# Activations computed in their result tiles, forget gates started five steps later, projection banks six and mixed banks two

## The chip, the cores and the metric

The kernel runs on one core of one Trainium2 chip. The metric is the device time of one execution in microseconds (us): the median of several executions, here 3062.44 us over three (3062.06 to 3065.12). A profiled execution is a run of its own and has its own time.

## What is computed

Two layers of a hybrid model on one sequence of 1024 tokens of width 2048, all in fp32. One layer, cut to what matters:

```python
mod = silu(c) @ w_mod + b_mod                      # shift, scale, gate
h = rms_norm(x, g_pre) * (1 + scale) + shift
proj = h @ w_in                                    # a_q a_k a_v | s_u s_v | c_q c_k c_v c_g | z
y_a = sliding_window_attention(rope(a_q), rope(a_k), a_v, sinks)    # 16 heads of 64, 4 of keys
y_b = chunked_spatial_gating(gelu(s_u), gelu(s_v), ...)             # 8 groups, chunks of 128
log_alpha = log_sigmoid(c_g @ gla_w_gate_up + gla_b_gate) / 16      # the forget gates
y_c = rms_norm(gated_linear_attention(c_q, c_k, c_v, log_alpha))    # 4 heads
y = concat(y_a, y_b, y_c) * silu(z)
x = x + gate * rms_norm(y @ w_out, g_post)
```

`gelu` is the tanh form; `silu(z)` is computed as z (1 + tanh(z/2)) / 2, with the factor of a half put elsewhere.

## The kernel before

**Phases.** There are four phases, one for each of the two layers and the two halves of the sequence (512 tokens): `in_phase` computes the projections and all mixers of a half, `out_phase` the output projection. The time is set by TensorE (PE), which runs the projections as three matmuls for one product: weights and activations are each split into a rounded high part and the rest, and high by high, high by rest and rest by high are summed in one PSUM bank (`mm_f`, L378, with the features on the partitions; `mm_t`, L386, with the tokens). Each group of projections (`group`, L394) has four result tiles of 128 x 512, each with a PSUM bank of its own from the pool `pj`, and runs over the 16 blocks of the inner dimension: for each block, one step of three matmuls into each of the four tiles. A group has 64 such steps. The order of the groups in a phase is `kcq`, `ck`, `vcg`, `q0`, `cv`, `q1`, `zc`, `sv`, `su`, `zb`, `za0`, `za1` and then four of the output; the first phase computes `kcq` and `ck` in a stage of its own at the start, together with the modulation vector.

**Weights.** Each weight block is loaded by a DMA of the SP queue, cast to its high part on ScalarE (ACT, L368), and the rest is taken on VectorE (DVE, L369); `w_take` keeps some blocks ready ahead.

**Lanes.** All else is written as generators that stand in lanes named `mod`, `att`, `gla`, `sg` and `fin`. After each projection step `tick` (L82) is called, and each lane whose time has come goes on to its next `yield`; the number it yields says after how many ticks it is called again. So a lane's matmuls are laid between those of the projections:
- `gla` first takes the forget gates (`gates`, L566): four transposes of the `c_g` columns of the value tiles (L569), a copy (L571), two matmuls (L576) and the elementwise work; then `gla_scores` (L593), twice, with small matmuls that fill two mixed banks at once (`far` at L649 with L655, `near` at L633) and are read by predicated copies (L620); then `gla_blocks` (L697: L712 and L715 into one bank, L722 into another); then the output transposes (L559).
- `att` takes four pairs of heads twice in a phase (`attention`, L473): two score tiles at once (L490), read by a ScalarE copy (L499, or L497 at the start of the sequence) and a predicated VectorE copy (L500), then softmax (L505 to L519), transposes (L532), and the product with the values (L546).
- `sg` mixes the gated part (L892); `mod` computes the modulation of what is to come during the first two phases.

All these matmuls write banks of the pool `mx`. PSUM has eight banks in this kernel, five for `pj` and three for `mx`.

**Order.** The order of instructions on each engine is not that of the source. A planner at compile time simulates the engines, and at each moment gives an engine the earliest instruction in the source whose inputs and tile it believes ready; `urgent` and `high_priority` move instructions ahead in this. A pool with n buffers gives out n tiles; the next one waits until one is released by its last reader. On the chip each engine then takes its own instructions strictly in the planned order, and waits where the planner was too hopeful.

**Activations.** After a group the results leave PSUM by `evac` (L761, copies on ScalarE, L767), `silu2` (L425) or `gelu2` (L431). The last two compute with scratch tiles of the pool `t2`, which has four buffers and serves many others as well (the rotary tables, gates, residual rows). Results go into tiles of the pool `hold`, which has 16 buffers, or, for `zb`, into a `t2` tile.

Of the kernel before, what the change touches and what calls it, by code (L numbers as in the profile page):

```python
# [15 lines left out]
AF = mybir.ActivationFunctionType  # L16
ALU = mybir.AluOpType
AX = mybir.AxisListType
PSUM = bass.MemoryType.PSUM
# [20 lines left out]
def hybrid_kernel(ctx: ExitStack, tc: tile.TileContext, a, y_out):  # L40
# [6 lines left out]
    whl_p = ctx.enter_context(tc.tile_pool(name="whl", bufs=4))  # L47
    t2_p = ctx.enter_context(tc.tile_pool(name="t2", bufs=4))
    sm = ctx.enter_context(tc.tile_pool(name="sm", bufs=2))
    pj = ctx.enter_context(tc.tile_pool(name="pj", bufs=5, space=PSUM))  # L50
    mx = ctx.enter_context(tc.tile_pool(name="mx", bufs=3, space=PSUM))
    pools = {}

    V, S, G, PE = nc.vector, nc.scalar, nc.gpsimd, nc.tensor

    def load(out, in_):
        nc.sync.dma_start(out=out, in_=in_)

    def urgent():
        return tc.high_priority(offset=PRIO)  # L60
# [32 lines left out]
    def hold(shape=(P, 512), dt=F32):  # L93
        return pools["hold"].tile(list(shape), dt, tag="hold", name="hold")

    def t2(shape=(P, 512), dt=F32):
        return t2_p.tile(list(shape), dt, tag="t2", name="t2")
# [7 lines left out]
    def mxt():  # L105
        return mx.tile([P, 512], F32, tag="mx", name="mx")

    def pjt():
        return pj.tile([P, 512], F32, tag="pj", name="pj")
# [13 lines left out]
    def rsqrt(out, src, n, pool=sm):  # L123

        i = pool.tile([P, n], I32, tag="rq_i", name="rq_i")
        V.tensor_scalar(i, src.bitcast(I32), 1, None, ALU.logical_shift_right)
        V.tensor_scalar(i, i, -1.0, 1597463007.0, ALU.mult, ALU.add)
        yv = i.bitcast(F32)
        for it in range(3):
            w = pool.tile([P, n], F32, tag="rq_w", name="rq_w")  # L130
            V.tensor_tensor(w, yv, yv, ALU.mult)
            V.scalar_tensor_tensor(w, w, -0.5, src, ALU.mult, ALU.mult)
            dst = out if it == 2 else yv
            V.scalar_tensor_tensor(dst, w, 1.5, yv, ALU.add, ALU.mult)
            yv = dst
# [288 lines left out]

    def silu2(dst, ps):  # L425

        t = t2()
        S.activation(t, ps, AF.Tanh, scale=0.5)
        V.scalar_tensor_tensor(dst, t, 1.0, ps, ALU.add, ALU.mult)

    def gelu2(dst, ps):  # L431

        x = t2()
        u = t2()
        with urgent():
            S.copy(x, ps)  # L436
        S.activation(u, x, AF.Square)
        V.tensor_scalar(u, u, 0.044715, 1.0, ALU.mult, ALU.add)
        V.tensor_tensor(u, u, x, ALU.mult)
        S.activation(u, u, AF.Tanh, scale=GELU_C)  # L440
        V.scalar_tensor_tensor(dst, u, 1.0, x, ALU.add, ALU.mult)

    y_d = [[dram.tile([P, 512], F32, name=f"y{h}_{j}") for j in range(NK)] for h in range(NH)]
    state = {}
# [119 lines left out]
            yield 3  # L564

    def gates(l, cg):  # L566
        tp = mxt()
        for n in range(NT):
            PE.transpose(tp[0:16, n * P:(n + 1) * P], cg[n], ident)  # L569
        cgT = t2()[32 * l:32 * l + 16, :]  # L570
        S.copy(cgT, tp[0:16, :])  # L571
        yield 9
        bs = []
        for i in range(2):
            ps = mxt()
            PE.matmul(ps, lhsT=wup[l][:, i * P:(i + 1) * P], rhs=cgT, start=True, stop=True)  # L576
            mn = t2()
            V.tensor_scalar(mn, ps, bgate[l][:, i:i + 1], 0.0, ALU.add, ALU.min)
            ab = t2()
            S.activation(ab, ps, AF.Abs, bias=bgate[l][:, i:i + 1])  # L580
            S.activation(ab, ab, AF.Exp, scale=-1.0)
            S.activation(ab, ab, AF.Ln, bias=1.0)
            V.scalar_tensor_tensor(mn, mn, CAP, ab, ALU.max, ALU.subtract)
            b = hold()
            for n in range(NT):
                c = slice(n * P, (n + 1) * P)
                V.tensor_tensor_scan(b[:, c], ones, mn[:, c], 0.0, ALU.mult, ALU.add)
            bs.append(b)
            yield 4
        yield 8  # L590
        return bs
# [162 lines left out]
    def in_phase(l, h, slots, pre=None):  # L754
# [61 lines left out]
        for n in range(NT):  # L816
            t = hold()
            with urgent():
                silu2(t, ps[n])
            zt.append(t)  # L820
# [14 lines left out]
        for n in range(NT):  # L835
            vn.append(hold())
            gelu2(vn[n], ps[n])
# [176 lines left out]
    with tc.tile_pool(name="start", bufs=1) as st:  # L1014

        load(mb[0], a["b_mod_col"][0])
        load(gpc[0], a["g_pre"][0])
        xq = [act_p.tile([P, 2, H], F32, tag="act", name="xq") for _ in range(8)]
        for c in range(8):
            load(xq[c], a["x_f"][0, 2 * c:2 * c + 2].rearrange("j p t -> p j t"))  # L1020
        scb = st.tile([P, NK, 32], F32, name="scb")
        V.tensor_copy(scb, sc.unsqueeze(2).broadcast_to([P, NK, 32]))
        ws, raw_q, hl_q = deque(), deque(), deque()

        def first_load(k):
            if k < NK:
                r = wraw_p.tile([P, 1, 768], F32, tag="wraw", name="wraw")
                load(r[:, 0, 0:512], a["w_in"][0, 0, :, k])
                load(r[:, 0, 512:], a["w_ck"][0, :, k])
                raw_q.append(r)  # L1030

        def first_split():
            r = raw_q.popleft()
            hl = whl_p.tile([P, 2, 1, 768], F32R, tag="whl", name="whl")
            S.copy(hl[:, 0], r)
            V.tensor_tensor(hl[:, 1], r, hl[:, 0].bitcast(F32), ALU.subtract)
            hl_q.append(hl)

        def mod_load(c, part):
            if c < 8:  # L1040
                w = st.tile([P, 8, 512], F32, name="wm0", bufs=3)
                load(w, a["w_mod"][0, c, :, 8 * part:8 * part + 8])
                ws.append(w)
        mod_load(0, 0)
        mod_load(0, 1)
        mod_load(1, 0)
        first_load(0)


        sums = mxt()  # L1050
        for c in range(8):
            sq = st.tile([P, 2, H], F32, name="sq", bufs=2)
            S.activation(sq, xq[c], AF.Square)
            s2 = st.tile([P, H], F32, name="s2", bufs=2)
            V.tensor_tensor(s2, sq[:, 0], sq[:, 1], ALU.add)
            PE.matmul(sums, lhsT=ones, rhs=s2, start=(c == 0), stop=(c == 7))
        r0 = st.tile([P, H], F32, name="r0")
        V.tensor_scalar(r0, sums, 1.0 / D, EPS, ALU.mult, ALU.add)
        rsqrt(r0, r0, H, st)
        psk = [mxt()] + [pjt() for _ in range(5)]  # L1060

        def project(k):
            first_split()
            if k >= NK - 2:
                w_load()
            hl = hl_q.popleft()
            for m in range(6):
                mm_f(psk[m], hl, 0, m, slots[k], k)

        def mod_products(mps, part):  # L1070

            w = ws.popleft()
            for kk in range(8):
                k = 8 * part + kk
                r = 32 * (k % 4)
                PE.matmul(mps[r:r + 32, :], lhsT=scb[:, k], rhs=w[:, kk], start=(k < 4), stop=(k >= 12))  # L1076

        def fill(c, mps):
            acc = st.tile([P, 512], F32, name="mod_acc", bufs=2)
            S.copy(acc, mps)  # L1080
            mod_columns(0, c, acc, 4)
            for j in range(2):
                k = 2 * c + j
                xt, b = t2(), bcol[0][:, k:k + 1]
                V.scalar_tensor_tensor(xt, xq[c][:, j], acol[0][:, k:k + 1], r0, ALU.mult, ALU.mult)
                s = act_p.tile([P, 2, 512], F32R, tag="act", name="act")
                S.activation(s[:, 0], xt, AF.Identity, bias=b)
                V.scalar_tensor_tensor(s[:, 1], xt, b, s[:, 0].bitcast(F32), ALU.add, ALU.subtract)
                slots.append(s)

        for c in range(8):
            if c:
                mod_load(c, 1)
                first_load(2 * c - 1)
            mps = mxt()
            mod_products(mps, 0)
            if c:
                project(2 * c - 2)  # L1100
                mod_load(c + 1, 0)
                first_load(2 * c)
            mod_products(mps, 1)
            with urgent():
                fill(c, mps)
            if c:
                project(2 * c - 1)
            if c == 5:
                for _ in rope_tables(0):
                    pass  # L1110
        first_load(NK - 1)
        project(NK - 2)
        project(NK - 1)
        w_split()
        w_split()
# [147 lines left out]
```

## Time and profile before

| | |
|---|---|
| time, median of 3 | 3062.44 us (3062.06 to 3065.12) |
| the profiled execution's own time | 3067.03 us |
| its span, first to last instruction | 3065.3 us |
| mean granted clock of TensorE | 0.993 |
| TensorE busy | 3000.0 us (98%), 17298 matmuls |
| VectorE busy | 1840.3 us (60%) |
| ScalarE busy | 1229.8 us (40%) |

In the profile PE is TensorE's matmuls and PEld its weight loads, DVE is VectorE, ACT is ScalarE, POOL is GpSimd and SP issues the DMAs. L382 is line 382 of the kernel before. A row of the waits names the instruction that waited, what it waited for, and the total, the number and the longest of these waits. A row of the timeline has the start, the duration, the engine and its instruction, `out<-in` by tile pool, and in brackets the idle time of the engine just before and what ended it. A row of one line's instructions has their shortest, median and longest duration in ns. A matmul's record lasts longer than the time to the next one, since matmuls overlap.

### The profile page before, as it was taken

The numbers are of one execution on the slowest core, as the hardware profiler recorded it, in microseconds if no ns is written. First come the engines' busy times: TensorE is split into PE (matmuls) and PEld (weight loads), VectorE is DVE, ScalarE is ACT, GpSimd is POOL, SyncE is SP. The second block draws the span as 40 slices with busy tenths as digits, with TensorE's granted clock in tenths as the row PEclk, the third lists the DMA queues.
The fourth block names the chain that finished last, engine by engine and source line by source line (L and its number), as shares of the span: only waits on it lengthen the run. The fifth ranks groups of instructions, "written<-read, shape, count | busy, mean of one in ns | idle before, by whom it ended". The sixth has DMA issues, their size and how long they took to land.

```text
span 3065.3 us, 44211 instructions
## 1 busy us (share of the span) xinstructions
PE 3000.0 (98%) x17298; PEld 2440.8 (80%) x17298; DVE 1840.3 (60%) x2948; ACT 1229.8 (40%) x2415; POOL 24.5 (1%) x66
## 2 busy tenths in 40 slices
PE   8999999999998999999999999999999999999998
PEld 4678777888886888788888788888888888888886
DVE  4668778464767877644364766644346476663425
ACT  3355455232434544323243554423223455442322
POOL 0000000000000000000000000000000000000000
PEclk9999999999999999999999999999999999999999
DMA  9744457475784445544455223334446322343535
GB/s 394 276 138 152 141 179 224 131 243 158 223 255 154 129 138 184 164 126 141 123 159 163 83 73 100 121 114 144 120 124 192 106 83 83 114 133 105 165 103 162
DMA packets 214914, 468.98 MB, mean 153 GB/s; under 512 B 21008, under 2 KB 72624, under 8 KB 212656
## 3 DMA queue, kind: packets, MB, share of 16 engines
q1 hardware_dynamic: 214704, 466.15, 48.6%
q8 instruction: 136, 2.23, 0.3%
q14 instruction: 74, 0.61, 0.1%
HBM read 429.37 MB, written 36.70 MB: 152 GB/s over the span
## 4 chain that ended last, share of the span: by engine, by line
PE 81%; DVE 8%; DMA 6%; ACT 3%; issue 2%; SPq 0%; DVEq 0%; ACTq 0%
PE pj L382 12%; PE pj L390 12%; PE pj L392 12%; PE pj L383 12%; PE pj L384 12%; PE pj L391 12%; DMA wm<-in_w_mod_dram 3%; PE mx L490 2%; PE mx L546 2%; DVE whl L369 2%; DVE ma L225 1%; PE mx L532 1%; ACT whl L368 1%; PE mx L1076 1%; DMA t<-in_x_dram 1%
## 5 line engine op out<-in xcount | busy, mean ns | idle before, releaser
L369 DVE TENSOR_TENSOR whl<-wraw,whl 128x1024 fp32r<-128x1024 f32 (+2 forms) x504 | 587.3, 1166 | 720.9 <-ACT whl L368 719.9
L368 ACT CAST whl<-wraw 128x1024 fp32r<-128x1024 f32 (+2 forms) x504 | 505.0, 1002 | 1048.3 <-PE pj L392 494.6
L390 PE MATMUL pj<-whl,act 128*128 128x512 f32 (+1 forms) x2048 | 785.0, 383 | 0.5 <-ACT hold L767 0.5
L392 PE MATMUL pj<-whl,act 128*128 128x512 f32 (+1 forms) x2048 | 778.5, 380 | 0.0
L391 PE MATMUL pj<-whl,act 128*128 128x512 f32 (+1 forms) x2048 | 775.9, 379 | 0.0
L382 PE MATMUL pj<-act,whl 128*128 128x512 f32 x1904 | 756.4, 397 | 9.1 <-ACT t L436 8.2
L383 PE MATMUL pj<-act,whl 128*128 128x512 f32 x1904 | 744.2, 391 | 0.0
L384 PE MATMUL pj<-act,whl 128*128 128x512 f32 x1904 | 742.6, 390 | 0.0
L392 PEld LDWEIGHTS pj<-whl,act 128*128 128x128 f32 x2048 | 385.6, 188 | 72.2 <-issue 0.3
L390 PEld LDWEIGHTS pj<-whl,act 128*128 128x128 f32 x2048 | 386.3, 189 | 70.8 <-issue 2.5
L391 PEld LDWEIGHTS pj<-whl,act 128*128 128x128 f32 x2048 | 386.0, 188 | 67.0 <-issue 0.8
L382 PEld LDWEIGHTS pj<-act,whl 128*128 128x128 f32 x1904 | 358.5, 188 | 100.4 <-issue 14.3
L384 PEld LDWEIGHTS pj<-act,whl 128*128 128x128 f32 x1904 | 358.6, 188 | 76.5
L383 PEld LDWEIGHTS pj<-act,whl 128*128 128x128 f32 x1904 | 358.9, 188 | 70.7 <-issue 0.7
L225 DVE SCALAR_TENSOR_TENSOR ma<-wm,sc,ma 128x512 f32<-128x512 f32 x240 | 179.9, 750 | 61.6 <-DMA wm<-in_w_mod_dram 58.7
L516 ACT ACTIVATE M<-M,at_nm 128x128 f32<-128x128 f32 x256 | 99.6, 390 | 19.4 <-DVE at_nm L508 19.4
L535 DVE TENSOR_TENSOR PT<-mx,amask 128x1024 f32<-128x1024 f32 x64 | 77.8, 1221 | 17.1 <-PE mx L532 17.0
L500 DVE COPY_PREDICATED M<-pmask,mx 128x256 f32<-128x256 uint8 x128 | 51.2, 442 | 53.5 <-ACT M L499 41.5
L490 PE MATMUL mx<-kc,qs 128*128 128x256 f32 (+1 forms) x256 | 66.2, 288 | 10.5 <-DVE hold L620 5.9
L490 PE MATMUL mx<-kc,qlo 128*128 128x256 f32 (+1 forms) x256 | 65.8, 285 | 0.0
L499 ACT COPY M<-mx 128x256 f32<-128x256 f32 x96 | 31.7, 375 | 80.7 <-PE mx L490 80.7
L490 PEld LDWEIGHTS mx<-kc,qs 128*128 128x128 f32 x256 | 49.3, 193 | 17.7 <-issue 7.1
(230 smaller groups left out, 2390.1 us busy)
## 6 DMA issues: line engine op xcount, KB each, us to landing
wraw<-in_w_in_dram SPq DMA_DIRECT2D x312, 512.0 KB, 3.6
wraw<-in_w_out_dram SPq DMA_DIRECT2D x136, 512.0 KB, 3.6
wm<-in_w_mod_dram SPq DMA_DIRECT2D x256, 256.0 KB, 3.7
wm<-in_w_mod_dram SPq DMA_DIRECT2D x16, 2048.0 KB, 13.7
y<-at SPq DMA_DIRECT2D x64, 256.0 KB, 2.9
q<-y SPq DMA_DIRECT2D x64, 256.0 KB, 2.8
q<-x SPq DMA_DIRECT2D x36, 256.0 KB, 2.7
wraw<-in_w_vcg_dram SPq DMA_DIRECT2D x32, 272.0 KB, 2.8
```

The source lines that it names most:

```text
L225: V.scalar_tensor_tensor(acc, ws[k], sc[:, k:k + 1], acc, ALU.mult, ALU.add)
L368: S.copy(hl[:, 0], raw)
L369: V.tensor_tensor(hl[:, 1], raw, hl[:, 0].bitcast(F32), ALU.subtract)
L382: PE.matmul(ps, lhsT=whi, rhs=slot[:, 0], start=(k == 0), stop=False)
L383: PE.matmul(ps, lhsT=whi, rhs=slot[:, 1], start=False, stop=False)
L384: PE.matmul(ps, lhsT=wlo, rhs=slot[:, 0], start=False, stop=(k == NK - 1))
L390: PE.matmul(ps, lhsT=slot[:, 0, c], rhs=whi, start=(k == 0), stop=False)
L391: PE.matmul(ps, lhsT=slot[:, 0, c], rhs=wlo, start=False, stop=False)
L392: PE.matmul(ps, lhsT=slot[:, 1, c], rhs=whi, start=False, stop=(k == NK - 1))
L490: PE.matmul(sps[p][:, b, k0:], lhsT=qi[:, p, n * P:(n + 1) * P], rhs=kc[2 * j + p][:, n * P + k0:n * P + 256], start=(part == 0), stop=(pa ...
L516: S.activation(Mf[:, k], Mf[:, k], AF.Exp, bias=nm[:, k:k + 1], scale=0.125, accum_out=den[:, k:k + 1])
L535: V.tensor_tensor(pt, tp.rearrange("p (n q) -> p n q", n=NT).unsqueeze(1).broadcast_to([P, 2, NT, P]), amask.unsqueeze(2).broadcast_to([P, ...
```

## The change

`silu2` writes its tanh into the destination and multiplies there. `gelu2` copies the projection straight into its destination and computes the result there, with one scratch tile in place of two. The generator `gates` begins with a `yield 5`. The pool `pj` has six banks and `mx` two; in the first stage the six accumulators, which were one `mx` and five `pj` tiles, are all of `pj`.

```diff
-    pj = ctx.enter_context(tc.tile_pool(name="pj", bufs=5, space=PSUM))
-    mx = ctx.enter_context(tc.tile_pool(name="mx", bufs=3, space=PSUM))
+    pj = ctx.enter_context(tc.tile_pool(name="pj", bufs=6, space=PSUM))
+    mx = ctx.enter_context(tc.tile_pool(name="mx", bufs=2, space=PSUM))
...
     def silu2(dst, ps):
 
-        t = t2()
-        S.activation(t, ps, AF.Tanh, scale=0.5)
-        V.scalar_tensor_tensor(dst, t, 1.0, ps, ALU.add, ALU.mult)
-
-    def gelu2(dst, ps):
-
-        x = t2()
-        u = t2()
+        S.activation(dst, ps, AF.Tanh, scale=0.5)
+        V.scalar_tensor_tensor(dst, dst, 1.0, ps, ALU.add, ALU.mult)
+
+    def gelu2(x, ps):
+
         with urgent():
             S.copy(x, ps)
+        u = t2()
         S.activation(u, x, AF.Square)
         V.tensor_scalar(u, u, 0.044715, 1.0, ALU.mult, ALU.add)
         V.tensor_tensor(u, u, x, ALU.mult)
         S.activation(u, u, AF.Tanh, scale=GELU_C)
-        V.scalar_tensor_tensor(dst, u, 1.0, x, ALU.add, ALU.mult)
+        V.scalar_tensor_tensor(x, u, 1.0, x, ALU.add, ALU.mult)
...
     def gates(l, cg):
+        yield 5
         tp = mxt()
...
-        psk = [mxt()] + [pjt() for _ in range(5)]
+        psk = [pjt() for _ in range(6)]
```

## The prediction

> **What bounds the kernel now.** I read the first part of the page, then the shares of the chain, then TensorE's waits by line, and then single stretches of the timeline.
>
> ```profile
> span 3065.3 us, 44211 instructions
> PE 3000.0 (98%) x17298; PEld 2440.8 (80%) x17298; DVE 1840.3 (60%) x2948; ACT 1229.8 (40%) x2415; POOL 24.5 (1%) x66
> PE 81%; DVE 8%; DMA 6%; ACT 3%; issue 2%; SPq 0%; DVEq 0%; ACTq 0%
> PE pj L382 12%; PE pj L390 12%; PE pj L392 12%; PE pj L383 12%; PE pj L384 12%; PE pj L391 12%; DMA wm<-in_w_mod_dram 3%; PE mx L490 2%; PE mx L546 2%; DVE whl L369 2%; DVE ma L225 1%; PE mx L532 1%; ACT whl L368 1%; PE mx L1076 1%; DMA t<-in_x_dram 1%
> ```
>
> TensorE is in the chain for 81% and idle for 65 us. The change takes no instruction away and adds none, so it can only win waits of TensorE or make new ones. These are the waits that can answer to it:
>
> ```profile
> engine line waited for: us in total, times, longest us
> PE pj L382 <- ACT t L436: 8.2, 6, 3.5
> PE mx L490 <- DVE hold L620: 5.9, 5, 2.3
> PE mx L569 <- ACT v L767: 5.5, 2, 3.0
> ...
> PE mx L633 <- DVE hold L620: 1.3, 1, 1.3
> ...
> PE pj L390 <- ACT hold L767: 0.5, 1, 0.5
> PE pj L382 <- DVE hold L995: 0.5, 1, 0.5
> ```
>
> Together they are 21.9 us. Idle time counts from the end of a record, and records overlap:
>
> ```profile
> 497.96 0.39 PE L382 MATMUL pj<-act,whl 128*128 128x512 f32 x1
> ...
> 498.64 0.39 PE L382 MATMUL pj<-act,whl 128*128 128x512 f32 x1
> ```
>
> One projection step is three matmuls, and the next step's L382 starts 0.68 us later: one matmul each 0.227 us, though each is recorded as 0.39. A wait seen as idle is therefore 0.16 us longer in truth (0.39 less 0.227). A step of 0.68 us is also one tick, the unit in which the lanes are spaced.
>
> **Part 1, gelu in place.** Before, the copy out of a projection bank (L436) goes into a t2 tile, of which there are four, and each gelu keeps two until its last VectorE operation. The third copy of a group must wait for the first gelu to end. The rotary-table lane can hold t2 tiles too.
>
> ```profile
> 503.60 0.59 ACT L436 COPY t<-pj 128x512 f32<-128x512 f32 x1 [1.48 <-PE pj L384]
> 504.76 0.57 ACT L436 COPY t<-pj 128x512 f32<-128x512 f32 x1
> ...
> 511.65 1.29 DVE L441 SCALAR_TENSOR_TENSOR hold<-t,t 128x512 f32<-128x512 f32 x2
> ...
> 512.37 0.58 ACT L436 COPY t<-pj 128x512 f32<-128x512 f32 x1 [1.11 <-DVE hold L441]
> ...
> 513.00 0.80 PE L382 MATMUL pj<-act,whl 128*128 128x512 f32 x1 [3.54 <-ACT t L436]
> ```
>
> Two copies run as soon as their banks are full; the third starts 7.6 us after the second, right after the first L441, and TensorE, already in the next group, stands for 3.54 us until its bank is read. ScalarE's own wait says the same:
>
> ```profile
> L436 ACT COPY t<-pj x32: 562/568/588, 456.3 to 2747.0; 128x512 f32<-128x512 f32 x32
> ...
>   DVE hold L441: 9.1, 8
> ```
>
> After, the copy goes into the hold tile that is the result, and only the square keeps a t2 tile. By the code some 8 of the 16 hold tiles are taken when the `sv` group ends and 10 when `su` ends, so a hold tile is free. Removed: 8.2 + 6 x 0.16 = 9.2 us. I leave 0.5, since the first copies of `sv` still queue behind the attention's exponentials on ScalarE: **-8.7**. Bounds: -9.2, and -4.5 if half of it only changes to a wait for ScalarE's queue. The silu in place frees a t2 tile and shortens no instruction: 0. Its cover is that none of the waits above has L428 or L429 as its cause.
>
> **Part 2, five steps ahead of the gates.** The gates' four transposes (L569) come one tick into `q0` and need the evacuated `v` tiles. In the first two phases these copies stand in ScalarE's queue behind a weight cast that waits for its DMA.
>
> ```profile
> 159.84 0.29 PE L392 MATMUL pj<-whl,act 128*128 128x272 f32 x1
> 159.97 0.39 PE L382 MATMUL pj<-act,whl 128*128 128x512 f32 x1
> ...
> 161.94 1.04 ACT L368 CAST whl<-wraw 128x1024 fp32r<-128x1024 f32 x1 [3.08 <-DMA wraw<-in_w_in_dram]
> 162.90 1.24 ACT L767 COPY v<-pj 128x272 f32<-128x272 f32 x4
> 163.32 1.17 PE L569 MATMUL mx<-ident,v 128*16 128x128 f32 x4 [2.50 <-ACT v L767]
> ```
>
> Five ticks are 3.4 us, so the transposes now come at about 160 + 3.4 = 163.4, when the first copy has landed. But the wait does not vanish with them. Those same copies free the projection banks. With six banks four are held by `vcg`, so `q0` can start two tiles; its third is due at 159.97 + 2 x 0.68 = 161.3 and waits for the first copy until 163.3, that is 2.0 us. What is won is one tile's step (0.68) and the spacing of the four transposes, which took 1.17 us because each waited for a copy (an estimate of 0.4 back to back: 128 columns each at the rate of 512 in 0.227, so 4 x 0.06, and a record's tail of 0.16): 0.68 + 0.8 = 1.5 in each of these two phases, **-3.0**. Bounds: 0 if the third tile and the late transposes wait as long as now, and -5.5 - 2 x 0.16 - 2 x 0.8 = -7.4 if the order lets other projections by. The lane then runs 3.4 us late for the whole phase. It issues no DMA on the way; it ends in `sv`, some 170 ticks (over 110 us) ahead of where it is drained, so its lateness costs nothing in itself.
>
> **Part 3, six projection banks.** The two small bank waits (0.5 and 0.5, with 0.16 each) go: **-1.3**. Bounds -1.3 and 0. The first stage is unchanged: its accumulators take six projection banks in place of five and one, and two mixed banks rotate there as before.
>
> **Part 4, two mixed banks.** The trace has no two-bank run, so this is bounded by evacuations.
>
> ```profile
> L499 ACT COPY M<-mx x96: 353/373/383, 228.0 to 2688.0; 128x256 f32<-128x256 f32 x96
> ...
> L500 DVE COPY_PREDICATED M<-pmask,mx x128: 425/442/455, 225.2 to 2688.5; 128x256 f32<-128x256 uint8 x128
> ...
> L620 DVE COPY_PREDICATED hold<-gmask,mx x160: 278/296/731, 202.1 to 2529.6; 32x128 f32<-32x128 uint8 x128, 64x512 f32<-64x512 uint8 x16, 64x256 f32<-64x256 uint8 x16
> ```
>
> ```profile
> 222.07 0.76 PE L633 MATMUL mx<-hold 64*32 64x32 f32 x64
> ...
> 223.15 2.04 DVE L620 COPY_PREDICATED hold<-gmask,mx 32x128 f32<-32x128 uint8 x8
> 223.56 0.23 PE L490 MATMUL mx<-kc,qs 128*128 128x128 f32 x1
> ...
> 225.12 0.30 PE L490 MATMUL mx<-kc,qs 128*128 128x128 f32 x1 [0.24 <-DVE hold L620]
> ```
>
> Here is the collision of now: a pair of gate-score tiles (L633), one tick later a pair of attention-score tiles (L490), whose second tile has no third bank left. All of these cost 5.9 + 1.3 and six times 0.16, about 8.2 us, and I count 8.0 as gone, because five ticks more take each L633 pair and the pair of L649 behind an L490 pair instead of just ahead of it. What comes: counted by ticks, one phase then has
> - L633 one tick behind an L490 pair, which is free after two copies and one predicated copy (0.37 + 0.37 + 0.44 = 1.2): 1.2 - 0.68 = 0.5;
> - L649 in the same tick as an L490 pair: 1.2;
> - the value product L546 one tick behind the second L633 of the other half, whose first tile takes 4 x 0.296 = 1.2: 0.5;
> - the output transposes L559 one tick behind L490 pairs, twice about 0.45: 0.9;
> - the third of the tiles that L692, L715 and L722 take in one tick: 0.6.
>
> That is 3.7 us a phase and 14.8 in all if nothing slips past. The planner does move projections ahead of a blocked tile where it foresees the wait, so I take three quarters, nearer the full count because it did not foresee those 8.2: +11. Term: -8 + 11 = **+3**. Bounds: -8 (all foreseen) and, if the old collisions also stay, +14.8.
>
> **Sum.** -8.7 - 3.0 - 1.3 + 3.0 = -10.0. The profiled execution took 3067.0 (span 3065.3 and 1.7 around it), 4.6 over the median of 3062.4; so 3057.0 for such an execution and 3052.4 for the median.
>
> **Rivals.**
> 1. *All waits go.* The planner fills the bank waits. Of the new ones a quarter stays: -9.2 - 7.4 - 1.3 - 8 + 3.7 = -22.2: 3040. For it: the six projection lines hold 12% of the chain each, so there is always a projection that could go first. Against it: the third tile of `q0`, and that today's bank waits were not foreseen.
> 2. *The gain is given back in the banks.* The old collisions only change places and the full 14.8 comes: -8.7 - 3.0 - 1.3 + 14.8 = +1.8: 3064, no change. The same result comes if the hold tile that a copy now needs is not free, for then the stop of part 1 stays. For it: VectorE's and ScalarE's queues hold weight splits of 1.2 and 1.0 us (L369, L368) that any evacuation may meet. Against it: the lanes are moved apart.
> 3. *Slower: each pair waits for the pair before it.* A score pair, L633 or L649 takes both banks, so nothing can be computed while it is read. There are 64 score pairs (512 matmuls by 8), 16 of L633 and 8 of L649, 88. Against the other 21 us of gain (8.7 + 3.0 + 1.3 + 8) they break even at 0.24 us each; at 0.45, which is one predicated copy, they cost 40: 3062.4 - 21 + 40 = 3081. For it: a weight split ahead of the copy makes 1.2 us into 2.3, more than the three ticks (2.0 us) between a head's two pairs. Against it: today most pairs find their banks free, with only one more.
>
> The rule for this rival stands in the Trainium skill, Perfetto Trace Analysis, section Matmuls: independent groups should rotate through different banks, so that one is evacuated while the next is computed. For the projections the change follows it; for users that take two tiles at once two banks leave nothing to rotate. By that rule alone the time would be that of rival 3. The trace agrees as far as it goes: with three banks the second tile, not the first, is the one that waited at 225.12.
>
> **Chances.** Forecast 50%, rival 1 17%, rival 2 20%, rival 3 13%. No change means within 0.2%, which is 6.1 us and about what can be told here: 3056.3 to 3068.5. Of the forecast some 7 points fall into it (part 4 at its upper end). Faster: 43 + 17 = 60%; same: 7 + 20 = 27%; slower 13%. Range: from 3039, just under rival 1, to 3067, a little over rival 2; rival 3 is left out.
>
> **What would show it.** L436's wait for L441 and TensorE's wait for L436 gone (part 1 right); L569 without a wait but L382 of `q0` waiting for the `v` copies, about 2 us in the first two phases (part 2 right; no such wait means rival 1); L995 and L767 gone from TensorE's list (part 3); new waits of L490, L546, L559 or L649 for L499, L500 or L620 of about 11 us in all (part 4). Over 20 us of these, or TensorE waits for a copy into a hold tile, would make the forecast wrong.

## The result, and the profile after

The changed kernel takes 3050.5 us (median of 6, 3046.9 to 3055.4), the kernel before 3064.6 beside it (median of 6): ratio 0.9950, 95% interval 0.9939 to 0.9961, so 12 to 19 us less. The forecast was 10 us less (3052.4). The kernel is faster, by half as much again as forecast, and the time lies in the range.

The first part of the page after, and TensorE's waits after. The lines of the kernel have moved up by one or two: L382 is unchanged, L488 was L490, L530 was L532, L544 was L546, L548 was L550, L619 was L620, L648 was L649, L766 was L767.

```profile
span 3047.4 us, 44148 instructions
PE 2993.1 (98%) x17298; PEld 2437.1 (80%) x17298; DVE 1841.0 (60%) x2948; ACT 1228.1 (40%) x2415; POOL 27.4 (1%) x66
```

```profile
PE mx L530 <- DVE M L517: 5.4, 5, 1.5
PE pj L382 <- ACT v L766: 3.8, 2, 2.3
PE mx L648 <- issue: 2.9, 1, 2.9
...
PE pj L390 <- issue: 2.2, 1, 2.2
PE mx L488 <- ACT qs L468: 2.2, 2, 1.5
PE mx L488 <- ACT at L548: 1.9, 1, 1.9
PE mx L488 <- DVE M L498: 1.8, 4, 1.0
PE mx L544 <- DVE hold L619: 1.5, 1, 1.5
...
PE mx L557 <- DVE M L498: 0.3, 1, 0.3
```

The engines do the same work as before. L436's wait (8.2), the small bank waits (0.5 and 0.5), the second L490 tile's wait for L620 (5.9) and that of L633 (1.3) are gone; L569's wait (5.5) has become a wait of L382 for the same copies (3.8); and there are waits for mixed banks of 1.9 + 1.8 + 1.5 + 0.3 = 5.5, where the second of these kinds (L490 for L500) stood at 1.5 before.

To see where this happens I sum two stretches over the four phases. The mixers' stretch runs from the first matmul of `q0` to the first of `su`; the activations' stretch from there to the first of `za0`. Their edges are the 192 projection matmuls of each group, counted in the trace. The sums below have the length in us first. Before, mixers and then activations:

```profile
sum 1158.80, PE 1134.61 PEld 924.41 DVE 826.72 ACT 595.40 POOL 9.21; mean PE 283.65 PEld 231.10 DVE 206.68 ACT 148.85 POOL 2.30
sum 375.20, PE 366.51 PEld 298.81 DVE 227.86 ACT 150.28 POOL 8.21; mean PE 91.63 PEld 74.70 DVE 56.97 ACT 37.57 POOL 2.05
```

After:

```profile
sum 1155.00, PE 1133.88 PEld 920.60 DVE 826.10 ACT 597.71 POOL 9.26; mean PE 283.47 PEld 230.15 DVE 206.53 ACT 149.43 POOL 2.31
sum 363.40, PE 362.01 PEld 298.19 DVE 229.43 ACT 145.66 POOL 11.02; mean PE 90.50 PEld 74.55 DVE 57.36 ACT 36.42 POOL 2.75
```

Of the 17.9 us by which the span is shorter, 11.8 lie in the activations' stretch, 3.8 in the mixers', and 2.3 elsewhere. So the question for the runs is which part won the 11.8, and what lies behind the small 3.8.

A stop of TensorE can cost more than its idle time. The traces record the clock granted to TensorE, and in spells of about 3.4 us, now and then two or three in a row, it is one half. Here is the spell behind the stop of 3.54 us that the prediction shows in part 1 (its window, its length, what each engine did, and then the clock, 0.50), and TensorE in the spell and after it:

```profile
512.46:515.87 3.41, 2.87 (x7) 2.29 (x8) 3.36 (x7) 2.23 (x4) 0.00 (x0) 0.50 0.76 208
```

```profile
514.88 0.63 PE L382 MATMUL pj<-act,whl 128*128 128x512 f32 x1
515.30 0.63 PE L383 MATMUL pj<-act,whl 128*128 128x512 f32 x1
...
516.73 0.39 PE L382 MATMUL pj<-act,whl 128*128 128x512 f32 x1
516.96 0.39 PE L383 MATMUL pj<-act,whl 128*128 128x512 f32 x1
```

In the spell one matmul starts 0.42 us after another, behind it 0.23 us; so a spell full of projections costs up to 1.7 us, half of its length. In the mixers' stretch these spells add up to 23.9 us before and 10.2 after, in the activations' stretch to 3.4 and none: up to 6.8 and 1.7 us of the differences above are the clock's, and on an even clock the mixers' stretch would be up to 3.0 us longer after than before. Each of these ten spells (one of them of double length) begins during a stop of TensorE of 1.2 us or more, or less than 2 us after its end. Not every stop has one: there is none behind the 2.3 us at 910.8 in the kernel after. What decides it, these runs do not show.

### The profile page after: what moved, and what is told of

Its sections match the earlier page's. It is cut to its first block, busy times and chain, and to the rows that moved or that the text cites. A ratio compares the mean times of both kernels' runs of the same rounds, so it can differ in the third digit from the quotient of the medians.

```text
span 3047.4 us, 44148 instructions
## 1 busy us (share of the span) xinstructions
PE 2993.1 (98%) x17298; PEld 2437.1 (80%) x17298; DVE 1841.0 (60%) x2948; ACT 1228.1 (40%) x2415; POOL 27.4 (1%) x66
## 5 line engine op out<-in xcount | busy, mean ns | idle before, releaser
L390 PE MATMUL pj<-whl,act 128*128 128x512 f32 (+1 forms) x2048 | 782.7, 382 | 2.2 <-issue 2.2
L382 PE MATMUL pj<-act,whl 128*128 128x512 f32 x1920 | 760.7, 396 | 6.5 <-ACT v L766 3.8
L382 PEld LDWEIGHTS pj<-act,whl 128*128 128x128 f32 x1920 | 360.6, 188 | 106.0 <-issue 24.0
L390 PEld LDWEIGHTS pj<-whl,act 128*128 128x128 f32 x2048 | 386.0, 188 | 69.7 <-issue 3.0
L498 DVE COPY_PREDICATED M<-pmask,mx 128x256 f32<-128x256 uint8 x128 | 51.3, 441 | 42.3 <-ACT M L497 30.9
L488 PE MATMUL mx<-kc,qs 128*128 128x256 f32 (+1 forms) x256 | 67.6, 294 | 6.1 <-ACT qs L468 2.2
L488 PE MATMUL mx<-kc,qlo 128*128 128x256 f32 (+1 forms) x256 | 66.0, 283 | 0.1
L544 PEld LDWEIGHTS mx<-PT,v 128*64 128x64 f32 x960 | 52.5, 137 | 14.3 <-issue 6.5
L967 DVE SCALAR_TENSOR_TENSOR hold<-hold,ro,t 128x512 f32<-128x512 f32 x56 | 41.3, 750 | 36.9 <-DMA t<-in_x_dram 19.2
```

The source lines that it names most:

```text
L382: PE.matmul(ps, lhsT=whi, rhs=slot[:, 0], start=(k == 0), stop=False)
L390: PE.matmul(ps, lhsT=slot[:, 0, c], rhs=whi, start=(k == 0), stop=False)
L488: PE.matmul(sps[p][:, b, k0:], lhsT=qi[:, p, n * P:(n + 1) * P], rhs=kc[2 * j + p][:, n * P + k0:n * P + 256], start=(part == 0), stop=(pa ...
L544: PE.matmul(yp[64 * p:64 * p + 64, n * P:(n + 1) * P], lhsT=vv[:, g * 64:g * 64 + 64], rhs=pts[p][:, w, n], start=(w == 0), stop=(w == 1 o ...
```

## The experiments

Each run has 5 rounds beside the kernel before. The differences in us are the ratio times the median of the kernel before in that comparison (3064 to 3068); their intervals are about 3 to 4 us to either side. In the table, the two stretches are the sums worked out as above, each from one profiled execution, and the last column is the time at half clock in the mixers' stretch. In the activations' stretch only the kernel before and e2 have such a spell, of 3.4 us each.

| kernel | in place | five ticks | banks 6/2 | ratio (95%) | us | mixers | activations | half clock |
|---|---|---|---|---|---|---|---|---|
| before | | | | 1 | 0 | 1158.8 | 375.2 | 23.9 |
| e1 | x | | | 0.9971 (0.9959 to 0.9982) | -8.9 | 1158.0 | 364.7 | 20.5 |
| e2 | | x | | 0.9969 (0.9956 to 0.9982) | -9.5 | 1149.9 | 372.7 | 6.8 |
| e3 | | | x | 0.9976 (0.9967 to 0.9984) | -7.4 | 1166.9 | 362.9 | 23.9 |
| e4 | x | | x | 0.9980 (0.9971 to 0.9989) | -6.1 | 1160.5 | 362.8 | 17.1 |
| e5 | x | x | | 0.9935 (0.9923 to 0.9947) | -19.9 | 1148.2 | 364.0 | 10.2 |
| e6 | | x | x | 0.9961 (0.9949 to 0.9973) | -12.0 | 1157.5 | 362.2 | 10.2 |
| after | x | x | x | 0.9950 (0.9939 to 0.9961) | -15.3 | 1155.0 | 363.4 | 10.2 |

**e1, in place alone.** Of the diff, only `silu2` and `gelu2`:

```diff
-        x = t2()
-        u = t2()
+        u = t2()
...
-        V.scalar_tensor_tensor(dst, u, 1.0, x, ALU.add, ALU.mult)
+        V.scalar_tensor_tensor(x, u, 1.0, x, ALU.add, ALU.mult)
```

> Only the activations in place; five and three banks, gates not spaced. Theory (the terms of the prediction add up): the copies out of the banks no longer wait for a scratch tile, -8.7 us against the kernel before, and L436's wait for L441 gone. Rival (it needs the sixth bank too, because ScalarE's queue is late all the same): about -4.5 us, and TensorE still waits for L436 at the start of the su and zb groups.

Measured -8.9 us, and 10.5 us less in the activations' stretch. TensorE's waits in this kernel (the gelu copy is L433 here, the bank wait for L620 is L618):

```profile
PE mx L488 <- DVE hold L618: 6.1, 5, 2.4
PE mx L567 <- ACT v L765: 5.9, 2, 3.0
...
PE pj L382 <- ACT hold L433: 0.5, 1, 0.5
```

The wait for the copy is down from 8.2 to 0.5, the residue that the prediction left; the other two stand as before. Part 1 does its work with five banks, the theory holds, and the rival falls.

**e2, five ticks alone.**

```diff
     def gates(l, cg):
+        yield 5
```

> Only the five ticks ahead of the gates. Theory: with five banks the second tile of q0 waits for the v copies, so the wait of 5.5 us only changes its name (about -1.5 us there), and the old collisions of the gate scores with the attention scores, 8 us, go: about -9 us. Rival (collisions only change places): -2 us or less.

Measured -9.5, the theory's number, and most of it in the mixers' stretch (1158.8 to 1149.9). Its way there is only in part the theory's: TensorE's time at half clock falls in that stretch from 23.9 to 6.8 us, worth up to 8.5, and the mean granted clock of the kernel's seven executions is 0.996, where that of the kernel before beside it is 0.993. The bank wait for L620 is gone from this kernel's list, and the wait at the start of `q0` has only changed its name, as its timeline shows (L768 is the `v` copy):

```profile
160.54 0.39 PE L384 MATMUL pj<-act,whl 128*128 128x512 f32 x1
161.60 1.05 ACT L368 CAST whl<-wraw 128x1024 fp32r<-128x1024 f32 x1 [2.73 <-DMA wraw<-in_w_in_dram]
162.55 1.24 ACT L768 COPY v<-pj 128x272 f32<-128x272 f32 x4
162.99 0.50 PE L382 MATMUL pj<-act,whl 128*128 128x512 f32 x1 [2.05 <-ACT v L768]
```

One tile of `q0` runs, and the second stands until the first `v` copy has read its bank.

**e3, the banks alone.**

```diff
-    pj = ctx.enter_context(tc.tile_pool(name="pj", bufs=5, space=PSUM))
-    mx = ctx.enter_context(tc.tile_pool(name="mx", bufs=3, space=PSUM))
+    pj = ctx.enter_context(tc.tile_pool(name="pj", bufs=6, space=PSUM))
+    mx = ctx.enter_context(tc.tile_pool(name="mx", bufs=2, space=PSUM))
...
-        psk = [mxt()] + [pjt() for _ in range(5)]
+        psk = [pjt() for _ in range(6)]
```

> Only the banks, six and two. Theory: the small bank waits go (-1.3), the wait for L441 shrinks by the spare bank (about -2), and the collisions of before, now without a third bank, grow from 8 to about 20 us: together +5 to +10 us. Rival (the planner lays projections into the bank waits): -3 us, or no difference.

Measured -7.4: the theory falls, and not for the rival's reason. Its waits of TensorE:

```profile
PE mx L490 <- DVE hold L620: 7.9, 3, 6.5
PE mx L569 <- ACT v L767: 7.5, 2, 4.3
...
PE pj L382 <- ACT t L436: 0.3, 1, 0.3
```

and from the view of the gelu copy, what ScalarE waited for:

```profile
L436 ACT COPY t<-pj x32: 560/569/590, 458.2 to 2742.6; 128x512 f32<-128x512 f32 x32
...
  DVE hold L441: 10.6, 10
```

The copy still waits for the scratch tile, 10.6 us on ScalarE where it was 9.1; but TensorE no longer stands for it (0.3, where it was 8.2), since the next group has the spare bank for the tile that would have waited. So one more bank wins what the copy in place wins: 12.3 us in the activations' stretch, against 10.5. In the mixers' stretch two mixed banks do cost what was feared, 8.1 us more (1158.8 to 1166.9, with the same time at half clock), with one stop of 6.5 us behind a late L620.

**e4, in place and banks.** The kernel after without `yield 5`.

> The kernel after without the five ticks: in place and banks. Theory: -8.7 and -1.3 of the first and third part, and the collisions stay and grow: about 0 us against the kernel before, 14 us slower than the kernel after. Rival (planner fills the waits; the spacing is worth only what it saves at the start of q0): -9 to -12 us, within 5 us of the kernel after.

Measured -6.1, between the two. The sum of the theory counted part 1 and the bank as two gains; the activations' stretch (362.8) shows that they are one. The mixers' stretch costs 1.7 more than before and 5.5 more than in the kernel after.

**e5, in place and spaced, five and three banks.** The kernel after with the banks of before.

> The kernel after with five and three banks: in place and spaced. Theory: what the two mixed banks cost comes back (the bank waits of 5.5 us that the kernel after shows) and the sixth projection bank is lost (1.3 us, and 1.4 us in q0): about 3 us faster than the kernel after. Rival (the sixth bank is worth more than the third mixed one): 3 us slower than the kernel after or more.

Measured -19.9: the fastest of these, and 4.6 below the kernel after by ratio (the intervals overlap), as the theory had it. The activations' stretch is 0.6 longer than in the kernel after, the mixers' stretch 6.8 shorter (1155.0 to 1148.2):

```profile
sum 1148.20, PE 1134.62 PEld 925.70 DVE 825.76 ACT 595.20 POOL 9.34; mean PE 283.66 PEld 231.43 DVE 206.44 ACT 148.80 POOL 2.33
```

**e6, spaced and banks.** The kernel after without the activations in place.

> The kernel after without the activations in place: spaced, six and two banks. Theory: the stall of the third copy stays, less by what the sixth bank covers (0.7 us each time): about 7 us slower than the kernel after. Rival (the sixth bank covers most of it): within 3 us of the kernel after.

Measured -12.0, 3.3 short of the kernel after; the intervals overlap, so in place adds little once the sixth bank is there. This is nearer to the rival (within 3) than to the theory (7), and agrees with e3.

**e7, the `v` copies on VectorE**, in the kernel after.

```diff
-        vt = evac(4, lambda: pools["v"].tile([P, 272], F32, tag="v", name="v"), ps)
+        vt = []
+        with tc.high_priority(offset=600):
+            for m in range(4):
+                t = pools["v"].tile([P, 272], F32, tag="v", name="v")
+                V.tensor_copy(t, ps[m])
+                vt.append(t)
```

> The kernel after with the four copies of the value projections on VectorE in place of ScalarE. Theory (ScalarE's queue holds them behind a weight cast that waits for its DMA, and the third tile of q0 waits for their bank): the 3.8 us that TensorE waits for these copies go, -3 to -4 us against the kernel after. Rival (VectorE's queue is as late, its weight split stands behind the same cast): no difference, or up to 2 us slower.

Measured -6.7 (0.9969 to 0.9987 around 0.9978), so about 9 us slower than the kernel after. The rival's mechanism, and worse than it said. Timeline at the start of `q0`; L790 is the copy:

```profile
161.45 1.04 ACT L368 CAST whl<-wraw 128x1024 fp32r<-128x1024 f32 x1 [3.66 <-DMA wraw<-in_w_in_dram]
...
162.77 1.22 DVE L369 TENSOR_TENSOR whl<-wraw,whl 128x1024 fp32r<-128x1024 f32 x1
163.90 1.48 DVE L790 COPY v<-pj 128x272 f32<-128x272 f32 x4
164.39 0.50 PE L382 MATMUL pj<-act,whl 128*128 128x512 f32 x1 [3.19 <-DVE v L790]
```

The copies now stand behind the weight split, which waits for the cast, which waits for the DMA: TensorE's wait for them is 7.6 us where it was 3.8. The mixers' stretch is 1160.6, 5.6 more than in the kernel after; the waits are 3.8 more, and 17.1 us at half clock in place of 10.2 are worth up to 3.4. The rest of the 9 lies within the intervals or is not accounted for.

**e8, ten ticks**, in the kernel after: `yield 10`.

> The kernel after with ten ticks in place of five. Theory (what counts is that the gate lane does not meet the attention lane; by ticks ten is no better than five): within 3 us of the kernel after. Rival (the particular five is what wins, the rest is chance of the order): 5 us or more slower than the kernel after.

Measured 0.9944 (0.9932 to 0.9956), -17.2: within 2 us of the kernel after, with 1151.2 in the mixers' stretch (10.2 at half clock). The particular five is not what wins.

**e9, e11 and e10, side by side on one chip:** the kernel after once more, e5 once more, and e5 with ten ticks.

> The kernel after, unchanged, on one chip with the next two. Both theories: -15 us against the kernel before, as it had.

> The kernel after with five and three banks again (as in the kernel that left only the banks as they were), beside the kernel after. Theory (with the copies in place and the gates spaced the sixth projection bank has nothing left to win, and the third mixed bank still has): 4 to 5 us faster than the kernel after. Rival (the two are the same and the chips differed): no difference.

> In place, five and three banks, ten ticks in place of five. Theory (with three banks hardly a collision is left, so the distance does not matter): within 3 us of the same kernel with five ticks. Rival (more distance is better at three banks too): 3 us faster or more.

Measured 0.9951 (0.9937 to 0.9965), 0.9929 (0.9917 to 0.9941) and 0.9926 (0.9914 to 0.9937); medians 3050.7, 3044.4 and 3044.3. Against the kernel after, five and three banks win 6 us (by the ratios 6.7), after 4.6 in e5; the intervals still overlap a little (0.9937 against 0.9941). Ten ticks and five are the same there. The stretches of the two kernels that were run again are 1156.8 and 362.8 (e9; 1155.0 and 363.4 in the kernel after) and 1148.0 and 364.7 (e11; 1148.2 and 364.0 in e5), with 13.7 and 6.8 us at half clock in the mixers' stretch: a difference of 2 us between two stretches tells nothing. So the version that beats the kernel before, and the kernel after in both comparisons, is the change without its banks.

## Why the prediction was right, and where not

**Part 1** (-8.7) was right, alone: -8.9 in e1, by the wait that was named, with the half microsecond that was left. In its stretch it won more, 10.5: the idle time that went (7.7), 0.8 for five records' ends, and up to 1.7 for the spell at half clock behind the stop of 3.54 us. The prediction has no term for the spell, though the row it shows at 513.00 lasts 0.80 us in place of 0.39.

**Part 2** was right in its main claim: the wait does not vanish with the transposes, it passes to the third tile of `q0`. The timeline after:

```profile
160.07 0.39 PE L382 MATMUL pj<-act,whl 128*128 128x512 f32 x1
...
160.77 0.40 PE L382 MATMUL pj<-act,whl 128*128 128x512 f32 x1
...
161.66 1.04 ACT L368 CAST whl<-wraw 128x1024 fp32r<-128x1024 f32 x1 [3.78 <-DMA wraw<-in_w_in_dram]
162.61 1.24 ACT L766 COPY v<-pj 128x272 f32<-128x272 f32 x4
163.04 0.50 PE L382 MATMUL pj<-act,whl 128*128 128x512 f32 x1 [1.43 <-ACT v L766]
```

Two tiles run, the third starts at 163.04; it was due at 161.45, so it waits 1.6 us, where 2.0 was forecast; in the second phase the wait is 2.3 us of idle time, so 2.5. Of the term of 3.0 the trace shows 2.9: 1.7 less idle time (5.5 to 3.8), and 1.2 by the four transposes, which take 0.60 us in both phases, where they took 1.17 and 1.24. The two spells at half clock that stood behind L569's waits before (at 164.3 and 922.1) are gone as well, up to 1.7 us each; they are in no term.

**Part 3** (-1.3) was wrong as a term, and this is the step that failed: each edit's gain was taken from the waits by name, as if the waits had one cure each. The wait for L436 needs a tile for the copy and a bank for TensorE, and either one ends it: -10.5 or -12.3 in that stretch, not both (e1, e3, and e4 with 362.8). The sum held because the change has both and I gave all of it to part 1. For the kernel with both, the sixth bank is worth about 0.6 us in that stretch (364.0 without it, 363.4 with it; 1.9 in e11 and e9), and perhaps part of the 2.3 elsewhere.

**Part 4** (+3) had the mechanisms in part and a size too large. The old collisions went with the spacing alone: in e2 the bank waits of 5.9 and 1.3 are gone, and the mixers' stretch became 8.9 us shorter. But the time at half clock fell there by 17.1 us, worth up to 8.5; what the collisions cost by themselves and what they cost through the clock behind them, the runs do not separate. The two banks then cost 6.8 (1148.2 to 1155.0, with 10.2 us at half clock in both) where 11 was forecast, and even that is not all waiting for banks: TensorE's list has 5.5 us of such waits after and 2.7 in e5 (2.5 of L488 and 0.2 of L654, both for L498), a difference of 2.8, and stops of another kind (the last section) more than make up the rest. Of the 5.5 only 1.8 are of the kinds that were counted by ticks (L544 for L619 and L557 for L498); the score pairs' waits for the pair before (L488 for L498, 1.8) and for the copy of the attention's output (L488 for L548, 1.9) were not in that count. A wait that was in it is the value product one tick behind the second L633:

```profile
1035.78 2.03 DVE L619 COPY_PREDICATED hold<-gmask,mx 32x128 f32<-32x128 uint8 x8
...
1037.75 0.98 PE L544 MATMUL mx<-PT,v 128*64 128x128 f32 x14 [1.48 <-DVE hold L619]
```

It was priced at 0.5 for each phase and came once, at 1.5. With 6.8 in place of 11 the sum of the prediction is -14.2, and by the ratio the time moved by 15.3.

**The price of a stop** is the second step that failed: the prediction takes it as the idle time and 0.16 us. Of the 17.9 us between the two profiled executions up to 8.5 (6.8 and 1.7) are the time at half clock that went, and against them stand 5.1 us of stops that the prediction does not have (the last section). That the sum comes so near without either is in part luck.

**Rivals.** Rival 1 (all waits go, -22) did not come with this kernel; e5 comes near it by taking back the banks, not by the planner filling them. One half of rival 2's mechanism, the old collisions staying, is seen in e4, though the time there is 6 us better than the kernel before. Rival 3 (every pair waits for the one before) did not come: in e3, where its condition is met without spacing, the mixers' stretch grew by 8.1, which is 0.09 us for each of the 88 pairs against the 0.24 from which it decides. The rule of the Trainium skill beside it (Perfetto Trace Analysis, Matmuls: rotate independent groups through different banks) holds for both pools as a direction, and says nothing of the size: a bank more wins 12.3 and 10.5 us in the activations' stretch where the gelu copies wait for a scratch tile (before to e3, e2 to e6), and 1.9 and 0.6 where they do not (e1 to e4, e5 to the kernel after); a bank less makes the mixers' stretch 2.5 (e1 to e4) to 8.1 us longer.

## What to carry to other kernels

When an engine waits for an evacuation, ask what the evacuation itself waits for: a scratch tile in the way and a missing bank show as the same row, and one cure is enough. Then do not pay for the second: here the sixth bank bought almost nothing that the copy in place had not bought, and the kernel that gives it a bank of the mixers is 5 to 7 us slower than the one that does not. Count a long stop of TensorE twice: as idle time, and, where the clock record shows a spell at half clock behind it, as up to half of that spell. And a wait that is moved off one instruction is found again at the next one that needs the same thing, here the bank that the late copies were to free.

## What had not been expected

TensorE stops inside or right behind the runs of small gate-score matmuls, with no semaphore to wait for that the profile shows. In the kernel after, a run of L648 is followed by a gap of 2.9 us, and in that gap (260.2 to 263.1) the DMA view shows one block on the instruction queue:

```profile
263.08 0.23 PE L648 MATMUL mx<-hold 64*16 64x16 f32 x7 [2.91 <-issue]
```

```profile
q8 instruction: 1, 0.02, 1.9%
```

The second stop after (2.2 us, at L390 behind L648) and one of the kernel before have such a block as well:

```profile
2500.78 1.24 PE L649 MATMUL mx<-hold 64*64 64x64 f32 x94
2503.77 0.24 PE L649 MATMUL mx<-hold 64*16 64x16 f32 x10 [1.75 <-issue]
```

A stop belongs to the planned order and not to the execution: of those over 1 us, two stand at the same work in the kernel before and in e1 (3.0 and 3.1 us in all), two others in the kernel after, in e6, in e7 and in e9 (4.7 to 5.4), and none in the other runs. What one costs is seen best in the third phase, here of the kernel after and then of e5 (the window in the mixers' stretch, its length, what each engine did, the clock):

```profile
1661.30:1944.50 283.20, 280.58 (x2063) 228.71 (x2062) 185.82 (x328) 146.03 (x349) 3.51 (x16) 0.99 0.31 94
1659.00:1938.20 279.20, 279.14 (x2063) 228.60 (x2062) 185.92 (x328) 145.74 (x349) 3.53 (x16) 1.00 0.31 95
```

The 4.0 us between them are the stop of 2.2 and half of the 3.4 us at half clock right behind it (from 1758.5); in the fourth phase, where neither kernel has a stop of this kind or a spell, the kernel after is 0.9 shorter (280.4 against 281.3). So about 5 of the 6.8 us that the kernel after loses against e5 are its own stops. Of the 8.8 between e9 and e11 the stops (5.4) and the clock (up to 3.4) can be all. For the banks themselves that leaves some 0 to 2 us at five ticks. They cost more at ten, where neither kernel has one of these over 1 us: 1151.2 us in the mixers' stretch with six and two (e8), 1144.2 with five and three (e10), and up to 1.7 of these 7.0 are the clock's (10.2 us at half clock against 6.8). The stops of the kernel before were worth less than their length: in its fourth phase the one of 1.75 us is gone in e2, and the stretch is 0.6 shorter (281.9 to 281.3).

An instruction block that comes late would fit the stops, but blocks are loaded without a stop too (135 in the kernel after), and no run moved these matmuls by themselves; their cause stays open.
